# A two-block network on one core: the 32 x 32 inversions' data moved by TensorE, x normalized before its split, HGRN's levels copied under a mask

## The chip, the core and the metric

The kernel runs on one core of a Trainium2 chip. The metric is device time in microseconds of one execution: the median of the runs of the kernel before is 3642.4 us (three runs, 3641.06 to 3648.86 us). The engines are named as in the profile: PE is TensorE (PEld its weight loads), DVE is VectorE, ACT is ScalarE, POOL is GpSimd, SP is SyncE, which mostly issues DMAs. ACTq and SPq are DMA issues standing in the queues of ACT and SP.

## The reference

512 tokens of 1024 features pass through a first block (one layer, three branches) and a second block (two layers). The change touches the first block, up to the state space branch:

```
xn = rmsnorm(x, norm1_w);  p = xn @ w_in
z, xbc, dt, p_rwkv, p_hgrn, p_gate = split(p)
y_ssm  = ssd_branch(z, xbc, dt, ...) @ w_branch_ssm
y_rwkv = rwkv7_branch(p_rwkv, ...)   @ w_branch_rwkv
y_hgrn = hgrn2_branch(p_hgrn, ...)   @ w_branch_hgrn
mixed  = sigmoid(p_gate)[0] * y_ssm + [1] * y_rwkv + [2] * y_hgrn
x = x + mixed @ w_out;  then norm, feed-forward, norm, and the second block
# RWKV-7, per head of 64, both directions:
S_t = S_{t-1} diag(w_t) - (S_{t-1} kk_t)(kk_t a_t)^T + v_t k_t^T;  y_t = S_t r_t
# HGRN-2, per head of 128, both directions:
S_t = diag(f_t) S_{t-1} + (1 - f_t) v_t^T;  o_t = S_t^T q_t;  o = rmsnorm(o) * silu(g)
```

The kernel solves the RWKV recurrence in chunks of 64 tokens, for which it needs the inverse of a unit triangular 64 x 64 matrix (I + A) per chunk, head and direction: 32 of them in a tile of two heads.

## The kernel before, in words

All large products run on PE with the weights and the input each split into two float16 parts (three products for one). A 512 KB weight unit comes by DMA, ACT makes its high part (L1058 or L1054), DVE or POOL its low part (L1059, L1055).

`start` (L1374) loads x, and for each of its 8 tiles splits gain times x into the two parts xh and xl at once and adds up its squares. 1/rms comes out later: along the partitions as `rb`, by token as `rt`. The 1/rms is therefore multiplied into whatever the products give: in `conv_pad` (L247, DVE), in HGRN's q, k, i and g (L801, L806, L811, DVE), in the gates (L1310, POOL), in the z path of the state space branch.

The first layer (`first`, L914) has this order. RWKV (`rwkv`) is traced first, as foreground, four tiles j of two heads one after the other. For each, `rwkv_mid` (L396) makes G, all causal products of a chunk, under a mask; takes the 32 x 32 diagonal blocks of (I + A) out of G through a DRAM buffer `pd` into M, with a matrix per partition (issues L432, L441); inverts them by rows with DVE, in two independent chains of rows (L463 multiplies, L466 subtracts); sends the inverse X by DRAM buffer `pd2` back into G (L470, L473); and then completes the block above the diagonal with PE (L480 transposes, L485 and L490 products, copies by ACT and DVE to L491). `rwkv_scan` (L494) then walks over 8 chunks: PE products with the state z, DVE's L523 (minus the right side), PE by the inverse (L526), copies `uv`, and the next state: PE L533, DVE L541 adds the old state, DVE L542 multiplies by the decay. Inside chunk 2 of the scan, the next tile's projections (`rwkv_in`) are traced, inside chunk 4 its decays. `rwkv_out` (L555) ends a tile with a layer norm (PE transposes L580).

HGRN's four heads and 16 gate tiles are background: traced after RWKV in the order "hghhghgg" (h one head, g four gate tiles), with two PSUM banks "bg" of their own, and a scheduler moves their instructions into places where it expects engines to be idle. Each engine then executes its own list strictly in order. A head has seven levels, each with DVE products (L839, L840), PE products into the bank H (L845), and, for five of them, a DVE multiplication by a mask (L847) and a POOL addition (L848) into the score tile `hs`; then DVE's L859 and L860 for the next level.

When RWKV, the four heads and the 16 gates are through, the banks are given out again and the state space branch (`ssd`, L609, first product L625) begins, with one accumulator bank "acc"; its background is the two up projections of RWKV and HGRN, eight more gates and its own. Weight units come in two written lists, FOREGROUND and BACKGROUND.

## Time and profile before

| | us |
|---|---|
| median of three runs | 3642.4 |
| lowest and highest | 3641.06, 3648.86 |
| the profiled execution's span | 3644.9 |
| up to G of tile 0 (first L432) | 99.1 |
| RWKV's four tiles, to the last layer norm | 99.1 to 679.1 |
| first product of the state space branch | 687.6 |
| end of the state space branch, about | 985 |
| the rest: output, feed-forward, second block | 985 to 3644.9 |

A row of the timeline has a start, a duration, engine, line, operation, output<-input, how many run together, and in brackets the idle time before it with what ended it. In a view by line, the busy time and the mean length follow the bar, then the idle time before. A tile's name stands without its buffer number.

### The profile page before, as it was taken

Reading aid. Unit: us, or ns where it says so; the run is one execution under the profiler, and the core shown is the slowest. Engines: PE = TensorE matmul, PEld = TensorE weight load, DVE = VectorE, ACT = ScalarE, POOL = GpSimd, SP = SyncE. Lnnn points to the kernel's source line nnn. Section 1 sums busy time; section 2 is a strip of 40 time slices with the busy share of each in tenths; the row PEclk is TensorE's granted clock in tenths of the full one; section 3 lists DMA queues with packets and bytes.
Section 4 is the critical chain, followed back from the end, with each engine's and each line's share of the span. In section 5 each row is a group of like instructions: output and inputs, shape, how many; then the busy total and the mean of one; then the engine's idle time right before and its main releaser. Section 6 shows DMA issues by size and latency. Waiting matters only on the chain. (4 is left out here: it accounts for less than half of the span.)

```text
span 3644.9 us, 60827 instructions
## 1 busy us (share of the span) xinstructions
PE 3388.2 (93%) x23758; PEld 2045.0 (56%) x23758; DVE 2751.5 (75%) x5599; ACT 1624.4 (45%) x3033; POOL 751.7 (21%) x762
## 2 busy tenths in 40 slices
PE   7899898898899999999989999999999989999998
PEld 3566565554445567655545545568655545545567
DVE  6767867587577798688767677788688767767788
ACT  4232232455444444364456544444364456634344
POOL 1322223223332212101110131211101120132211
PEclk9897999999999999999999999999999999999999
DMA  4211212333352234322323353335322323353233
GB/s 137 70 49 40 64 40 63 131 111 113 106 171 94 97 99 142 108 74 75 106 76 100 106 170 99 98 112 159 106 73 72 105 81 101 108 172 123 94 99 98
DMA packets 151157, 368.17 MB, mean 101 GB/s; under 512 B 44098, under 2 KB 47428, under 8 KB 150868
## 3 DMA queue, kind: packets, MB, share of 16 engines
q1 hardware_dynamic: 117492, 336.03, 29.5%
q0 software_dynamic: 7680, 23.00, 1.9%
q10 hardware_dynamic: 25696, 5.25, 0.8%
q8 instruction: 186, 3.05, 0.3%
q14 instruction: 103, 0.84, 0.1%
HBM read 322.72 MB, written 40.04 MB: 100 GB/s over the span
## 5 line engine op out<-in xcount | busy, mean ns | idle before, releaser
L1169 PE MATMUL acc<-xh,whi 128*128 128x512 f16 x1224 | 469.3, 383 | 33.0 <-DVE w L753 11.8
L1171 PE MATMUL acc<-xh,wlo 128*128 128x512 f16 x1224 | 469.1, 383 | 20.6 <-DVE wlo L1059 20.3
L1170 PE MATMUL acc<-xl,whi 128*128 128x512 f16 x1224 | 469.6, 384 | 0.0
L1058 ACT ACTIVATE whi<-wst 128x1024 f16<-128x1024 f32 x240 | 250.0, 1049 | 263.4 <-PE acc L1170 141.7
L1059 DVE SCALAR_TENSOR_TENSOR wlo<-wst,whi 128x1024 f16<-128x1024 f32 x240 | 319.0, 1329 | 15.4 <-ACT whi L1058 14.9
L1169 PE MATMUL bg<-xh,bhi 128*128 128x512 f16 x788 | 311.1, 395 | 9.9 <-DVE hi L811 8.2
L1171 PE MATMUL bg<-xh,blo 128*128 128x512 f16 x788 | 310.5, 394 | 5.8 <-DVE reset L309 3.2
L1170 PE MATMUL bg<-xl,bhi 128*128 128x512 f16 x788 | 311.1, 395 | 0.0
L1171 PEld LDWEIGHTS <-wlo 128*128 128x128 f16 x1632 | 160.7, 98 | 232.5 <-DVE wlo L1059 46.4
L1170 PEld LDWEIGHTS <-whi 128*128 128x128 f16 x1632 | 160.5, 98 | 213.0 <-issue 41.6
L1169 PEld LDWEIGHTS <-whi 128*128 128x128 f16 x1632 | 161.1, 99 | 193.8 <-ACT whi L1058 13.5
L1428 POOL TENSOR_TENSOR w<-w,w 128x512 f32<-128x512 f32 x66 | 117.0, 1773 | 445.4 <-DVE w L1428 280.1
L1059 DVE SCALAR_TENSOR_TENSOR blo<-bst,bhi 128x1024 f16<-128x1024 f32 (+1 forms) x156 | 180.5, 1162 | 34.4 <-ACT bhi L1058 32.7
L1204 PE MATMUL acc<-whi,xh 128*128 128x128 f16 x1152 | 195.1, 219 | 2.1 <-DVE bias L1843 1.2
L1058 ACT ACTIVATE bhi<-bst 128x1024 f16<-128x1024 f32 (+1 forms) x156 | 136.4, 887 | 133.0 <-PE bg L1170 95.7
L1206 PE MATMUL acc<-whi,xl 128*128 128x128 f16 x1152 | 195.0, 219 | 0.0
L1205 PE MATMUL acc<-wlo,xh 128*128 128x128 f16 x1152 | 195.0, 219 | 0.0
L1171 PEld LDWEIGHTS <-blo 128*128 128x128 f16 x1172 | 117.0, 100 | 131.3 <-issue 16.3
L1170 PEld LDWEIGHTS <-bhi 128*128 128x128 f16 x1172 | 117.1, 100 | 130.7 <-issue 29.0
L1169 PEld LDWEIGHTS <-bhi 128*128 128x128 f16 x1172 | 117.3, 100 | 114.7 <-issue 15.1
L1204 PEld LDWEIGHTS <-xh 128*128 128x128 f16 x1408 | 139.9, 99 | 15.2 <-issue 5.0
L1205 PEld LDWEIGHTS <-xh 128*128 128x128 f16 x1408 | 140.0, 99 | 6.8 <-issue 5.0
(665 smaller groups left out, 9117.2 us busy)
## 6 DMA issues: line engine op xcount, KB each, us to landing
wst<-win SPq DMA_DIRECT2D x92, 512.0 KB, 3.6
bst<-win SPq DMA_DIRECT2D x64, 512.0 KB, 3.7
wst<-wff SPq DMA_DIRECT2D x60, 512.0 KB, 3.6
bst<-w SPq DMA_DIRECT2D x44, 512.0 KB, 3.5
gd<-bw SPq DMA_DIRECT2D x88, 256.0 KB, 2.1
ug<-gd SPq DMA_DIRECT2D x88, 256.0 KB, 2.7
wst<-w SPq DMA_DIRECT2D x34, 512.0 KB, 3.5
wst<-wf SPq DMA_DIRECT2D x30, 512.0 KB, 3.4
```

The source lines that it names most:

```text
L1058: nc.scalar.activation(out=hi[:, h], in_=st[:, h], func=AF.Copy, scale=WS)
L1059: nc.vector.scalar_tensor_tensor(out=lo[:, h], in0=st[:, h], scalar=WS, in1=hi[:, h], op0=ALU.mult, op1=ALU.subtract)
L1169: mm(ps, lhsT=wh, rhs=h[:, k, :], start=(k == 0), stop=False)
L1170: mm(ps, lhsT=wh, rhs=l[:, k, :], start=False, stop=False)
L1171: mm(ps, lhsT=wl, rhs=h[:, k, :], start=False, stop=(k == nk - 1))
L1204: mm(o, lhsT=xh, rhs=wh, start=(k == 0), stop=False)
L1205: mm(o, lhsT=xh, rhs=wl, start=False, stop=False)
L1206: mm(o, lhsT=xl, rhs=wh, start=False, stop=(k == 7))
L1428: tt = lambda eng, o, x, y, op=ALU.add: eng.tensor_tensor(out=o, in0=x, in1=y, op=op)
```

## The change

Six edits, all in the first block:

1. The inversion's data go by PE. G's 32 x 32 blocks are multiplied by parts of the identity into PSUM (64 products) and copied to M by four ACT copies. M and X now lie with the columns outside, so that a step along a row is 32 elements. The two chains become one, on all rows, with X padded by interleaved zero columns so that the rows of one half of the partitions count as even and the others as odd. X comes back by 16 products of 128 x 128 by 64 columns into PSUM, eight copies into G, and 32 small products with two copies into `st`, for which the transposes are gone. Both DRAM buffers and their DMAs are gone.
2. `start` adds up the squares first, then multiplies x by 1/rms (three tiles on POOL, five on DVE), then splits. What was multiplied by `rb` or `rt` later is now scaled by a constant, mostly in an ACT activation that reads PSUM.
3. HGRN's levels below the sixth: one predicated copy on DVE from PSUM into `hs` in place of the mask product and POOL's addition.
4. RWKV's old state is added in PSUM by a product with the identity; L523's work goes from DVE to ACT, and the two copies `uv` change engines.
5. The background is traced as "hhghghgg", its weight units with it.
6. The kernel is built with a DMA scratch size of 4096, and comments are gone, which moves line numbers.

```diff
 def conv_pad(self, ps, side):
-        nc.vector.tensor_tensor(out=xp[:, 2:T + 2], in0=ps, in1=self.rb, op=ALU.mult)
+        nc.scalar.activation(out=xp[:, 2:T + 2], in_=ps, func=AF.Copy, scale=IWS)
 def rwkv_mid(self, j):
-        pd = self.t(self.dram, [2, 32, 32, 32], "pd")
-        for q in range(2):
-            s = slice(32 * q, 32 * q + 32)
-            nc.scalar.dma_start(out=pd[q].rearrange("m i t -> i m t"), in_=G[s, :, s])
...
-            (nc.scalar, nc.sync)[q].dma_start(out=M[s], in_=pd.rearrange("q m i t -> (q m) i t"))
+        for u in range(2):
+            ps = self.b("S")
+            for t in range(16):
+                for q in range(2):
+                    s = slice(32 * q, 32 * q + 32)
+                    mm(ps[s, 32 * t:32 * t + 32], lhsT=G[:, :, 32 * q + 16 * u + t], rhs=self.ident[:, s], start=True, stop=True)
+            for h in range(2):
+                nc.scalar.copy(out=M[64 * h:64 * h + 64, 512 * u:512 * u + 512], in_=ps[0:64])
...
         for i in range(31):
...
-            for c, n in rs:
-                v.tensor_tensor(out=t, in0=X[c][:, 0:n, i:i + 1]..., in1=M[:, i:i + 1, ts]..., op=ALU.mult)
-            for c, n in rs:
-                v.tensor_tensor(out=X[c][:, 0:n, ts], in0=X[c][:, 0:n, ts], in1=t, op=ALU.subtract)
-        pd2 = self.t(self.dram, [2, 32, 8, 2, 2, 32], "pd2")
...
-        for q in range(2):
-            s = slice(32 * q, 32 * q + 32)
-            nc.scalar.dma_start(out=G[s, :, s], in_=pd2[q].rearrange("m r c e t -> (r c e) m t"))
+            v.tensor_tensor(out=t, in0=Xv[:, rs, i:i + 1]..., in1=Mv[:, i:i + 1, ts]..., op=ALU.mult)
+            v.tensor_tensor(out=Xv[:, rs, ts], in0=Xv[:, rs, ts], in1=t, op=ALU.subtract)
+        for k in range(8):
+            for h in range(2):
+                mm(px[:, 64 * k:64 * k + 64], lhsT=X[:, o:o + 128], rhs=self.ident[:, 64 * h:64 * h + 64], start=(h == 0), stop=(h == 1))
+        for k in range(4):
+            for q in range(2):
+                if q:
+                    nc.scalar.copy(out=dst, in_=src)
+                else:
+                    v.tensor_copy(out=dst, in_=src)
+        for i in range(32):
+            mm(pt[i // 16][0:32, ...], lhsT=Xv[:, i // 2 * 2 + 1], rhs=self.ident[:, 64 * (i % 2):64 * (i % 2) + 32], start=True, stop=True)
+        nc.scalar.copy(out=st[:, 0:16], in_=pt[0][0:32]...)
+        v.tensor_copy(out=st[:, 16:32], in_=pt[1][0:32]...)
...
-                nc.tensor.transpose(px[lo, 32 * n:32 * n + 32], G[lo, m, lo], self.ident[lo, lo])
-            nc.scalar.copy(out=st[lo], in_=px[lo])
 def rwkv_scan(self, j):
-            v.tensor_scalar(out=wn[lo], in0=pw[lo, 0:256], scalar1=-1.0, scalar2=None, op0=ALU.mult)
+            nc.scalar.activation(out=wn[lo], in_=pw[lo, 0:256], func=AF.Copy, scale=-1.0)
-            v.tensor_copy(out=uv[0][lo, chs[0]], in_=pu[lo, 0:128])
-            nc.scalar.copy(out=uv[1][lo, chs[1]], in_=pu[lo, 128:256])
+            nc.scalar.copy(out=uv[0][lo, chs[0]], in_=pu[lo, 0:128])
+            v.tensor_copy(out=uv[1][lo, chs[1]], in_=pu[lo, 128:256])
+                    if z is not None:
+                        mm(o, lhsT=self.ident, rhs=z[:, d], start=True, stop=False)
-                    v.tensor_tensor(out=zf, in0=z.rearrange("p d k -> p (d k)"), in1=pz[:, 0:256], op=ALU.add)
-                    v.tensor_tensor(out=four_v(zf), in0=four_v(zf), in1=zb, op=ALU.mult)
+                v.tensor_tensor(out=zn..., in0=pz[:, 0:256]..., in1=zb, op=ALU.mult)
 def ssd(self, yh, yl):
-            v.tensor_tensor(out=z, in0=pz, in1=self.rb, op=ALU.mult)
-            nc.scalar.activation(out=th, in_=z, func=AF.Tanh, scale=0.5)
-            v.scalar_tensor_tensor(out=z, in0=th, scalar=1.0, in1=z, op0=ALU.add, op1=ALU.mult)
+            nc.scalar.activation(out=z, in_=pz, func=AF.Tanh, scale=0.5 * IWS)
+            v.scalar_tensor_tensor(out=z, in0=z, scalar=1.0, in1=pz, op0=ALU.add, op1=ALU.mult)
 def hgrn(self, yd):
-            v.tensor_tensor(out=q, in0=self.fmx(it), in1=self.rb, op=ALU.mult)
+            nc.scalar.activation(out=q, in_=self.fmx(it), func=AF.Copy, scale=IWS)
...
-                    v.tensor_tensor(out=t, in0=po..., in1=hm[:, l:l + 1]..., op=ALU.mult)
-                    nc.gpsimd.tensor_tensor(out=sc, in0=sc, in1=t, op=ALU.add)
+                    v.copy_predicated(sc, hm[:, l:l + 1].bitcast(U16)..., po...)
 def first(self, next_gain):
-                for s in "hghhghgg":
+                for s in "hhghghgg":
 def gates(self, name, u0, n, gd, g0=0):
-                nc.scalar.copy(out=g, in_=ps)
-                nc.gpsimd.tensor_tensor(out=g, in0=g, in1=self.rb, op=ALU.mult)
+                nc.scalar.activation(out=g, in_=ps, func=AF.Tanh, scale=0.5 * IWS)
 def start(self, gain):
-                self.norm_tile(k, x[:, k], gain)
-            self.norm_end()
+                self.square_sums(k, x[:, k], None, eng=nc.vector)
+            self.norm_end(1.0)
+            for k in range(8):
+                (nc.gpsimd if k % 3 == 1 else nc.vector).tensor_tensor(out=x[:, k], in0=x[:, k], in1=self.rb, op=ALU.mult)
+                self.split(self.xh[:, k, :], self.xl[:, k, :], x[:, k], self.col(gain, k))
```

How the scheduler's lists move with it is shown at three places.

DVE in the first inversion, before: tx and X with their numbers are the products and rows of the two chains, M the matrix; L811 is an HGRN head's.

```order
L811 TENSOR_TENSOR hi_3874<-bg_3883,rt_15_148 128x512
L463 TENSOR_TENSOR tx_111_559<-X_113_561,M_558 128x29
L463 TENSOR_TENSOR tx_112_560<-X_114_562,M_558 128x27
L466 TENSOR_TENSOR X_113_561<-X_113_561,tx_111_559 128x29
L466 TENSOR_TENSOR X_114_562<-X_114_562,tx_112_560 128x27
L263 TENSOR_SCALAR i_1038<-i_1038 128x512
```

There a subtraction never stands right behind the product that it needs. The same place near the first inversion's end, after: L464 and L465 are the product and the subtraction of the one chain, L818, L827, L841 and L848 an HGRN head's, L1059 a weight's low part.

```order
L464 TENSOR_TENSOR tx_634<-X_635,M_563 128x78
L465 TENSOR_TENSOR X_635<-X_635,tx_634 128x13x6
L464 TENSOR_TENSOR tx_634<-X_635,M_563 128x70
L818 SCALAR_TENSOR_TENSOR hg_4083<-hg_4083,bg_4091 128x512
L465 TENSOR_TENSOR X_635<-X_635,tx_634 128x14x5
L827 TENSOR_TENSOR hs_4197<-H_4192,ident_75 128x512
L464 TENSOR_TENSOR tx_634<-X_635,M_563 128x56
L841 TENSOR_TENSOR hw_4212<-hq_3860,hp_3902 128x2x128x2
L465 TENSOR_TENSOR X_635<-X_635,tx_634 128x14x4
L1059 SCALAR_TENSOR_TENSOR blo_4382<-bst_4379,bhi_4381 128x512
L464 TENSOR_TENSOR tx_634<-X_635,M_563 128x45
L848 COPY_PREDICATED hs_4197<-hgm_3845,H_4204 128x512
```

Each pair is now dependent, and the background's operations stand between the two of a pair. 62 operations of the chain take the place of 120 small ones in pairs.

PE from RWKV's last layer norm (L580, its transposes) to the first product of the state space branch (L625), before; the rows with bg are background products.

```order
L580 MATMUL T_3726<-ident_75,M_3408 128x128
L1171 LDWEIGHTS blo_6349
L1171 MATMUL bg_6383<-xh,blo_6349 128x512
L1169 LDWEIGHTS bhi_6348
L1169 MATMUL bg_6383<-xh,bhi_6348 128x512
...
L1170 MATMUL bg_6420<-xl,bhi_6386 128x512
L1171 LDWEIGHTS blo_6387
L1171 MATMUL bg_6420<-xh,blo_6387 128x512
L625 LDWEIGHTS xh
```

Here 42 background products of 512 columns stand between the layer norm's first transpose and L625. After, a part of the same stretch, which ends at L631 (the same product as L625 above); L1204 to L1206 are products of HGRN's i and g by token, L825 the first of its score products.

```order
L1206 LDWEIGHTS xl
L1206 MATMUL bg_5904<-bhi_5792,xl 128x128
L825 MATMUL H_6005<-hq_5680,hw_6003 128x128 x4
L1169 LDWEIGHTS bhi_5898
L1169 MATMUL bg_6190<-xh,bhi_5898 128x512
...
L1170 MATMUL bg_6438<-xl,bhi_6406 128x512
L1171 LDWEIGHTS blo_6407
L1171 MATMUL bg_6438<-xh,blo_6407 128x512
L631 LDWEIGHTS xh
```

The stretch now holds 315 background products of 512 columns, 192 of 128 columns and 82 of an HGRN head's scores and states. RWKV's four tiles hold 57, 20, 125 and 83 background products in place of 128, 112, 126 and 192.

DVE from the last layer norm to the state space branch, before: L568 and L574 belong to the norm, L582 to the tile's gate, L614 and what follows to the state space branch.

```order
L568 TENSOR_SCALAR rs_658_3709<-mv_649_3684 128x8
L574 TENSOR_SCALAR M_3408<-M_3408,mv_649_3684,rs_658_3709 128x64 x8
L582 TENSOR_SCALAR w_3731<-T_3726,cols_77 128x512
L614 TENSOR_SCALAR dsk_6480<-cols_77 128x8
L1223 SCALAR_TENSOR_TENSOR w_3736<-w_3731,w_3735 128x512
```

All four heads have ended ahead of it. After, L574 and L580 are the norm's, L885 to L908 the end of the third head, and L811, L841 and L848 the fourth head, whose levels run on to the branch's first row.

```order
L574 TENSOR_SCALAR rs_646_3813<-mv_637_3788 128x8
L580 TENSOR_SCALAR M_3506<-M_3506,mv_637_3788,rs_646_3813 128x64 x8
L885 COPY hst_5498<-H_5494 128x128
L908 TENSOR_TENSOR hw_5524<-hw_5524,hg_5244 128x512
L811 TENSOR_SCALAR hp_5715<-hk_5716,hc_655_3848,hc_654_3847 128x512
...
L841 TENSOR_TENSOR hw_6025<-hq_5680,hp_5715 128x2x128x2
L848 COPY_PREDICATED hs_6010<-hgm_3845,H_6017 128x512
...
L620 TENSOR_SCALAR dsk_6496<-cols_77 128x8
```

So a whole head and the end of another moved behind RWKV's last tile. From the first block's feed-forward on, the lists of DVE, ACT and POOL are the same before and after.

## Rows read from the trace of the kernel before

**Rows 1.** Windows by stage: length, busy time (x instructions) of PE, PEld, DVE, ACT, POOL, granted clock

```profile
541.10:676.00 134.90, 114.29 (x949) 76.73 (x947) 88.18 (x251) 41.66 (x91) 43.77 (x29) 0.92 0.21 61
676.00:688.00 12.00, 11.46 (x47) 5.39 (x48) 5.46 (x13) 5.32 (x10) 4.74 (x9) 0.84 0.57 180
```

**Rows 2.** Timeline of the second tile's inversion: start, length, engine, line, operation

```profile
244.47 0.31 ACTq L432 DMA_DIRECT2D pd<-G  x1
256.65 0.28 DVE L463 TENSOR_TENSOR tx<-X,M 128x31 f32<-128x31 f32 x2
290.42 0.17 DVE L466 TENSOR_TENSOR X<-X,tx 128x8 f32<-128x8 f32 x1
295.31 0.93 ACTq L473 DMA_DIRECT2D G<-pd  x2
305.24 0.94 PE L485 MATMUL S<-w,G 32*32 32x32 f32 x24
314.51 0.57 ACT L491 COPY G<-S 32x512 f32<-32x512 f32 x1 [1.03 <-PE S L490]
381.79 0.28 DVE L551 TENSOR_TENSOR M<-M,S 64x128 f32<-64x128 f32 x1 [0.32 <-PE S L550]
```

**Rows 3.** Timeline, the same issue L432 in the first and the last tile

```profile
99.15 0.96 ACTq L432 DMA_DIRECT2D pd<-G  x2
541.06 0.31 ACTq L432 DMA_DIRECT2D pd<-G  x1
```

**Rows 4.** Waits of ACT, 0 to 692: total us, times, longest

```profile
ACT w L482 <- PE S L480: 64.9, 4, 26.5
```

**Rows 5.** Groups by line, 0 to 692: busy us, mean ns, idle before

```profile
L466 DVE TENSOR_TENSOR X<-X,tx 128x54 f32<-128x54 f32 (+13 forms) x240 | 48.8, 242 | 0.0
L463 DVE TENSOR_TENSOR tx<-X,M 128x54 f32<-128x54 f32 (+13 forms) x240 | 47.5, 237 | 0.0
L541 DVE TENSOR_TENSOR z<-z,S 128x256 f32<-128x256 f32 x24 | 10.0, 419 | 13.6 <-PE S L533 13.5
L848 POOL TENSOR_TENSOR hs<-hs,hw 128x512 f32<-128x512 f32 x20 | 36.0, 1800 | 73.4 <-DVE hw L847 48.6 <-DVE X L466 24.8
```

**Rows 6.** Line L1623, durations in ns min/median/max: half of its reads are strided

```profile
L1623 DVE TENSOR_TENSOR w<-acc,rb x16: 691/863/1052, 1780.8 to 3110.9; 128x512 f32<-128x512 f32 x16
```

**Rows 7.** Timeline of DVE: L257 needs L256's output, L1059 needs neither

```profile
104.30 0.74 DVE L256 SCALAR_TENSOR_TENSOR fr<-xp,cols,fr 128x512 f32<-128x512 f32 x1
105.07 0.75 DVE L257 SCALAR_TENSOR_TENSOR fr<-xp,cols,fr 128x512 f32<-128x512 f32 x1
105.74 1.22 DVE L1059 SCALAR_TENSOR_TENSOR wlo<-wst,whi 128x1024 f16<-128x1024 f32 x1
```

**Rows 8.** Timeline of PE: pace of products of 512 and of 128 columns

```profile
978.04 0.38 PE L1171 MATMUL bg<-xh,blo 128*128 128x512 f16 x1
978.25 0.38 PE L1169 MATMUL bg<-xh,bhi 128*128 128x512 f16 x1
102.56 0.22 PE L1204 MATMUL bg<-bhi,xh 128*128 128x128 f16 x1
102.62 0.22 PE L1205 MATMUL bg<-blo,xh 128*128 128x128 f16 x1
```

**Rows 9.** Timeline of PE: the last layer norm and the state space branch's first product

```profile
679.13 0.42 PE L580 MATMUL T<-ident,M 128*128 128x128 f32 x1
687.60 0.19 PE L625 MATMUL acc<-wdh,xh 128*128 128x32 f16 x1
```

**Rows 10.** Timeline of DVE: one level of an HGRN head to the next

```profile
152.59 0.68 DVE L839 TENSOR_TENSOR hw<-hq,hp 128x512 f32<-128x512 f32 x1
157.80 0.68 DVE L839 TENSOR_TENSOR hw<-hq,hp 128x512 f32<-128x512 f32 x1
```

**Rows 11.** Timeline, 10 to 40 us: the first use of the first product

```profile
37.54 0.69 DVE L247 TENSOR_TENSOR xp<-acc,rb 128x512 f32<-128x512 f32 x1 [1.00 <-PE acc L1171]
```

**Rows 12.** Waits of PE in the state space branch, 692 to 985: total us, times, longest

```profile
PE acc L1169 <- DVE w L753: 11.8, 5, 3.8
```

More of the change, by code (lines that the diff above doesn't have):

```diff
@@ L13 @@
 BF16 = mybir.dt.bfloat16
+U16 = mybir.dt.uint16
 AF = mybir.ActivationFunctionType
@@ L475, in rwkv_mid @@
+        for i in range(32):
+            mm(pt[i // 16][0:32, 32 * (i % 16):32 * (i % 16) + 32], lhsT=Xv[:, i // 2 * 2 + 1], rhs=self.ident[:, 64 * (i % 2):64 * (i % 2) + 32], start=True, stop=True)
+        nc.scalar.copy(out=st[:, 0:16], in_=pt[0][0:32].rearrange("p (i m) -> p i m", m=32))
+        v.tensor_copy(out=st[:, 16:32], in_=pt[1][0:32].rearrange("p (i m) -> p i m", m=32))
+        st = M[0:32].rearrange("p (m i) -> p m i", i=32)
         lo, hi = slice(0, 32), slice(32, 64)
@@ L631, in ssd @@
         for i in range(4):
-            v.scalar_tensor_tensor(out=da[:, i], in0=pd[:, 32 * i:32 * i + 32], scalar=self.rt[:, i:i + 1], in1=self.row("dtb"), op0=ALU.mult, op1=ALU.add)
+            v.scalar_tensor_tensor(out=da[:, i], in0=pd[:, 32 * i:32 * i + 32], scalar=IWS, in1=self.row("dtb"), op0=ALU.mult, op1=ALU.add)
         v.tensor_scalar(out=fl(da), in0=fl(da), scalar1=-1.0, scalar2=None, op0=ALU.mult)
```

73 lines of the change are left out of this document (32 added, 41 removed), and 2 rows, old and new, of the table BACKGROUND.

## The prediction

> **What bounds the kernel now.** I read the windows by stage first, then the timeline of one RWKV tile, then the waits and the groups by line in 0 to 692 us, and last the two lists of instructions side by side. Everything that changes lies ahead of about 985 us; behind it the lists of DVE, ACT and POOL are the same, so the prediction is a sum over RWKV's four tiles, the stretch between them and the state space branch, and that branch.
>
> In an RWKV tile no engine is full: in the last one DVE is busy 88 of 135 us and PE 114, and PE's busy time counts background products and a granted clock of 0.92 [rows 1]. A chain bounds it. A tile takes (541.06 - 99.15) / 3 = 147.3 us [rows 3]. In the second, the way from G into the inversion takes 244.47 to 256.65, 12.2 us, the inversion to 290.6, 33.9 us, the way back until the products above the diagonal begin 14.6 us (290.6 to 305.24), those products to 315.1, 9.9 us, the scan to 382.1, 67 us; another 15 us go by until the next tile's G [rows 2]. While the inversion runs, ACT's queue stands behind the DMA issues: four waits of 65 us in all, the longest 26.5 us [rows 4]. Behind the last tile little is left: from the last transpose of its layer norm to the state space branch's first product 679.13 to 687.60, 8.5 us [rows 9].
>
> **The tile, part by part.** Into M: both DMA legs (12.2 us) give way to 64 products of 32 columns and four copies. The nearest row has 24 such in 0.94 us, 0.039 each [rows 2], so 2.5 us; at the pace of 128-column products, 0.06 [rows 8], 3.8. The last two copies are 1.1 us by L491's 0.57 [rows 2], and I allow 1 to 2 us for the hand-overs between engines: about 5.7, a gain of 6.5 (4 to 8).
>
> The inversion: 120 operations become 62 with the same elements, 2856 of each kind in a tile. In the trace they are busy (48.8 + 47.5) / 4 = 24 us a tile [rows 5]; the two shortest forms, of 8 and 31 elements a row, run at 0.17 and 0.14 us [rows 2], so most of it is a fixed price, and 58 operations at 0.06 to 0.11 give back 3.5 to 6.4 us. Two things take from it. The steps are now 32 elements apart. The nearest row is L1623, of whose 16 executions 8 read in steps of 64 elements: 0.69 us without and 1.05 us with them [rows 6], 0.7 ns more for an element; 2 x 2856 x 0.7 is 4 us (6 if the write pays too). And each operation needs the one in front. A dependent pair has a pitch of 0.77 us where the next, independent one has 0.67 [rows 7]; 62 x 0.10 is 6.2 us at most, less where background stands between the two. Last, POOL gives back ground: its additions L848, 36 us, go [rows 5], so that fewer of DVE's operations run beside one of POOL's, which may help and is priced by no row here. I take 0 for the inversion, from -6 to +6.
>
> The Trainium skill (page "SBUF — State Buffer", section "Door 1: The DMA port swizzle (why `[64,N]` ≈ `[32,N]`)") says that an access which crosses into another 16-byte line pays a penalty and that four fp32 are what can be strided over freely: a rule against this change. By it every element of the strided operands would pay; the 0.691 and 1.052 us above agree in sign. By the rule with its penalty on reads and writes alike the 6 us hold rather than the 4, and the sum is 8 us later. The page "VectorE: DVE Perf Modes", section "The DRAIN you can't avoid", says that an operation does not begin until the one before has left the pipe, in which case two independent chains bought nothing; by it the 6.2 us would be 0, the inversion some 4 us shorter in a tile, and the sum 15 us earlier. The pitches of 0.77 and 0.67 do not bear it out fully, and the sum goes by them.
>
> Back from X: four DMAs out, two in, transposes and a copy (14.6 us) give way to 16 products of 64 columns (0.08 each by the pace above, 1.3 us), eight copies on two engines (4 x 0.57 at most, 2 us), 32 products of 32 columns (1.2), a copy (0.6) and hand-overs (1): 6, a gain of 8.5 (6 to 10). The products above the diagonal lose the second half's transposes and copy: 2 of 9.9 us (0 to 3).
>
> The scan: the old state's addition L541, 0.42 us, leaves the chain in six chunks [rows 5], with a dependent step 6 x 0.5 = 3 us; the two products that replace it are due before the chain's own and hide behind the waits for `uv` (if not, 12 x 0.06 to 0.16 us, at most 2). L523's move to ACT is even: ACT is free, with the DMAs out of its queue. More comes from PE: the list puts 285 background products of 512 columns into the four tiles where 558 stood, and at 0.215 us each [rows 8] that is 59 us less PE work, 15 a tile, of which most was in the scans and part in the chain's way. I take 10 us in all (4 to 14). The projections' `conv_pad` on ACT instead of DVE (0.69 us [rows 11], three a tile), and the rest: 2.5 us (0 to 4).
>
> Sum: 6.5 + 0 + 8.5 + 2 + 10 + 2.5 = 29.5 us a tile. Over the way from the first L432 to the last layer norm, 3.85 tiles' worth of 147 us by rows 3 and 9 less the start, that is 114 us. `start` normalizes x before its split, but the first projection no longer waits for `rb` at 37.54 [rows 11]: I take 3 us earlier (from 3 later to 4). The last layer norm's transpose moves from 679 to about 562.
>
> **What comes behind.** What left the tiles has not left the program. 315 background products of 512 columns at 0.215 us are 67.9 us, 192 of 128 columns at 0.055 to 0.06 are 11, 82 for HGRN at 0.06 to 0.16 are 9: 88 us of PE time (84 to 93) where 42 products stood [rows 8]. They are in PE's list ahead of the state space branch, and so must all end before it. In them runs HGRN's fourth head, whose levels took 5.2 us each [rows 10], seven levels and the parts around them about 50 us, with 2 to 15 products between the levels; I add 15 us for PE's waits on it: 103 (85 to 118). The branch then begins at 562 + 103 = 665 in place of 687.6, 23 us earlier.
>
> In the branch itself 12 `conv_pad` and one operation of the z path leave DVE, which PE waited for 11.8 us [rows 12]; but the single accumulator bank is now held until DVE has read it behind ACT's tanh. I take 4 us less (from 10 less to 8 more). HGRN's predicated copies and scaled activations shorten work that is not on the chain, except in the fourth head. The scratch size I cost at nothing, since no step of the chain hangs on it (2 us either way).
>
> Together: 23 + 4 = 27 us off the profiled 3644.9, 3618. That execution is 2.5 us above the median of the three runs, so 3616.
>
> The break-even lies at a gain per tile of (103 - 8.5 - 3 - 4) / 3.85 = 23 us.
>
> **The rivals.** Faster: the tile shortens by 38 (the upper ends of the scan and of the way into M and back, 5 us from the inversion), 146 us in all, and the stretch behind takes the 88 of PE's work and no more: 679 - 146 - 3 + 88 = 618, 70 us early, with the branch's 4 that is 3571. For it speaks that POOL's slowing of DVE goes; against it that half-full PE has a granted clock of 0.92 and 0.84 in these stretches [rows 1], which less background would not raise.
>
> Slower: the inversion on strided columns costs 5 us more instead of 0, since every one of 62 operations pays for step and dependence, and the scan gives only the 4 us of its addition. The tile then shortens by 6.5 - 5 + 8.5 + 2 + 4 = 16 us, 62 in all, and the stretch behind is still 103: 679 - 62 - 3 + 103 = 717, 29 us late, 3671 with the branch's 4 off less the 2.5. It decides from the 23 us per tile above. Speaking for it: a background that once filled the waits of a chain is now run by itself.
>
> It doesn't do what it says: the waits on the DMAs are hidden behind other work of the chain, and moving them by PE changes nothing. ACT's four waits and the empty 12 and 15 us in the timeline [rows 2, 4] speak against; it would give about 3642.
>
> **Chances.** The forecast 0.48, with 3595 to 3637 as its own range; faster rival 0.22 (3555 to 3595); slower rival 0.27 (3637 to 3690); no effect 0.03. The range, 3560 to 3665, leaves out the far ends of both rivals. A measurement tells 0.2%, 7.3 us, from no change: faster than 3635 are the fast rival and 0.40 of the forecast, 0.62; within 0.2% the forecast's last 0.08, the slower rival's first 0.04 and the no-effect case, 0.15; slower 0.23.
>
> **What would show it.** In the profile after: the way from G to the inversion's first operation 5 to 7 us, and from its last to the products above the diagonal about 6; ACT's 26 us waits gone. The inversion's length, 28 to 40 us, tells the strided price. The last layer norm's transposes at 545 to 580, the branch's first product at 650 to 680, and between them PE over 80% busy. It is wrong if a tile still takes over 125 us, if PE waits over 25 us for HGRN's last head, or if the branch takes more than its 297 us.

## The result and the profile after

The changed kernel takes 3673.6 us, the median of six runs (3665.7 to 3698.4), the kernel before in the same rounds 3644.5: a ratio of 1.0088, with a 95% interval of 1.0060 to 1.0117. It is slower by some 29 us where 27 us less were forecast, and it lies beyond the range of 3560 to 3665. The profiled execution spans 3676.5 us.

The windows of the changed kernel by stage, cut at its own four tiles (each from the first of its G products) and at the last layer norm's transposes. The columns are those of [rows 1]: the busy time of PE, PEld, DVE, ACT and POOL, the granted clock of TensorE, the busy share of the DMA engines and the GB/s that they moved.

```profile
95.40:226.70 131.30, 120.99 (x1113) 90.10 (x1112) 92.38 (x191) 41.82 (x90) 20.80 (x21) 0.90 0.09 29
226.70:347.10 120.40, 111.43 (x1078) 83.30 (x1077) 80.28 (x196) 41.69 (x93) 19.02 (x21) 0.96 0.09 32
347.10:480.50 133.40, 124.20 (x1055) 85.53 (x1054) 93.41 (x216) 48.02 (x107) 25.62 (x23) 0.97 0.13 45
480.50:601.50 121.00, 110.38 (x1114) 85.74 (x1114) 79.58 (x204) 35.85 (x79) 24.07 (x18) 0.96 0.08 27
601.50:704.30 102.80, 97.25 (x675) 56.69 (x676) 53.97 (x82) 38.45 (x74) 29.23 (x23) 1.00 0.40 138
```

And of the kernel before, cut at the same places:

```profile
87.40:228.20 140.80, 125.72 (x982) 83.03 (x982) 104.30 (x275) 41.08 (x92) 40.65 (x37) 0.92 0.20 57
228.20:380.60 152.40, 141.38 (x1057) 97.90 (x1056) 107.23 (x304) 42.18 (x92) 36.00 (x37) 0.85 0.16 42
380.60:519.90 139.30, 128.42 (x1032) 86.64 (x1031) 112.06 (x301) 44.34 (x97) 42.23 (x36) 0.95 0.21 60
519.90:676.30 156.40, 133.98 (x1037) 90.44 (x1036) 100.62 (x292) 44.02 (x95) 50.49 (x33) 0.88 0.20 57
676.30:687.60 11.30, 11.27 (x47) 5.28 (x47) 4.76 (x12) 4.81 (x9) 4.61 (x8) 0.84 0.56 178
```

The tiles went from 147.2 to 126.5 us in the mean, 82.8 us in all. The stretch behind them went from 11.3 to 102.8 us, 91.5 more, and the first tile begins 8.0 us later (95.4 for 87.4). So the state space branch starts 16.7 us later: the first product at 704.34 for 687.60 [rows 9].

```profile
602.88 0.27 PE L586 MATMUL T<-ident,M 128*128 128x128 f32 x1
704.34 0.18 PE L631 MATMUL acc<-wdh,xh 128*128 128x32 f16 x1
```

From there to the end it is 2972.2 us for 2957.3, and the branch itself has no part in that. Up to the row of 1/rms behind it (`rbs`) it takes 276.9 us for 278.7:

```profile
965.60 0.69 DVE L1297 COPY rbs<-T 128x512 f32<-128x512 f32 x1 [1.04 <-PE T L1296]
980.52 0.69 DVE L1297 COPY rbs<-T 128x512 f32<-128x512 f32 x1 [1.64 <-PE T L1296]
```

The rest, where the lists of DVE, ACT and POOL are the same, is 2695.3 us for 2678.6. Ten traces looked at, of these two kernels and of eight below, have 2678.6 to 2695.3 there, with before's the shortest and the change's the longest: e_rm below, whose ACT list behind the branch is the change's instruction for instruction, has 2685.3. So these 17 us are the spread of single traces and aren't shown to belong to the change. Of the 29 us between the medians, 16.7 are seen ahead of the branch, and where the others come from stays open. The 16.7 is itself a difference of two single traces: the kernel before with nothing but another scratch size began its branch 7 us earlier.

The second tile, as in [rows 2]: M's copies, the inversion from L464 to L465, the products above the diagonal L494 to L500, the scan's last addition L557.

```profile
245.90 1.17 ACT L438 COPY M<-S 64x512 f32<-64x512 f32 x2 [0.68 <-PE S L436]
247.10 0.21 DVE L464 TENSOR_TENSOR tx<-X,M 128x31 f32<-128x31 f32 x1 [3.09 <-ACT M L438]
285.67 1.26 DVE L465 TENSOR_TENSOR X<-X,tx 128x16 f32<-128x16 f32 x1
293.75 1.19 PE L494 MATMUL S<-M,G 32*32 32x32 f32 x32
301.03 0.57 ACT L500 COPY G<-S 32x512 f32<-32x512 f32 x1 [1.74 <-PE S L499]
348.01 0.28 DVE L557 TENSOR_TENSOR M<-M,S 64x128 f32<-64x128 f32 x1 [0.74 <-PE S L556]
```

The way back is 6.9 us for 14.6, the inversion 39.8 for 33.9, the scan 46.7 for 67. But the scan's pair of numbers sets a scan at one granted clock against a scan at another. The first two scans, before and then after the change:

```profile
173.60:229.90 56.30, 55.64 (x407) 39.06 (x406) 34.41 (x81) 23.34 (x66) 15.71 (x12) 1.00 0.13 43
315.10:382.10 67.00, 66.25 (x425) 48.30 (x423) 40.79 (x92) 20.44 (x59) 13.98 (x11) 0.80 0.03 9
```

```profile
165.30:227.90 62.60, 58.47 (x389) 43.83 (x388) 33.01 (x71) 20.92 (x58) 9.84 (x7) 0.84 0.03 9
301.60:348.30 46.70, 46.70 (x391) 36.72 (x389) 23.15 (x57) 17.47 (x49) 2.12 (x1) 1.00 0.06 22
```

Before's second scan, the one that the forecast read, ran at a granted clock of 0.80, and its first at 1.00; in the change it is the other way round. At 0.97 to 1.00, before has scans of 56.3, 55.9 and 53.3 us, the change 46.7, 47.7 and 48.6, 5 to 10 us less; and each kernel has one slower scan, of 67.0 and 62.6 us. In the mean it is 58.1 and 51.4.

ACT's wait L482 of [rows 4] is gone. In its place stands a smaller one: the eight copies back into G were to run on two engines at once, and run in turn.

```profile
ACT G L480 <- DVE G L482: 28.0, 11, 7.2
```

The groups by line, 0 to 704 us, to [rows 5]: half the inversion's operations with 90.2 us of busy time for 96.3, and the predicated copy in place of GpSimd's 36 us.

```profile
L465 DVE TENSOR_TENSOR X<-X,tx 128x126 f32<-128x126 f32 (+22 forms) x124 | 47.8, 385 | 2.5
L464 DVE TENSOR_TENSOR tx<-X,M 128x126 f32<-128x126 f32 (+22 forms) x124 | 42.4, 342 | 9.1 <-ACT M L438 6.8
L848 DVE COPY_PREDICATED hs<-hgm,H 128x512 f32<-128x512 uint16 x20 | 14.5, 725 | 2.2 <-PE H L847 1.9
```

### The profile page after: what moved, and what is told of

It reads as the page before. It is cut to its first block, busy times and chain, and to the rows that moved or that the text cites. A ratio compares the mean times of both kernels' runs of the same rounds, so it can differ in the third digit from the quotient of the medians.

```text
span 3676.5 us, 62122 instructions
## 1 busy us (share of the span) xinstructions
PE 3420.7 (93%) x24622; PEld 2086.6 (57%) x24622; DVE 2715.8 (74%) x5282; ACT 1657.0 (45%) x3103; POOL 691.4 (19%) x709
## 5 line engine op out<-in xcount | busy, mean ns | idle before, releaser
L1171 PE MATMUL acc<-xh,wlo 128*128 128x512 f16 x1224 | 470.3, 384 | 21.6 <-DVE wlo L1059 21.6
L1059 DVE SCALAR_TENSOR_TENSOR wlo<-wst,whi 128x1024 f16<-128x1024 f32 x240 | 318.2, 1326 | 32.4 <-ACT whi L1058 24.7
L1059 DVE SCALAR_TENSOR_TENSOR blo<-bst,bhi 128x1024 f16<-128x1024 f32 (+1 forms) x156 | 182.6, 1174 | 48.3 <-ACT bhi L1058 46.1
L1204 PE MATMUL acc<-whi,xh 128*128 128x128 f16 x1152 | 195.1, 219 | 1.9 <-DVE bias L1845 1.3
L1206 PE MATMUL acc<-whi,xl 128*128 128x128 f16 x1152 | 195.0, 219 | 0.0
L1169 PEld LDWEIGHTS <-bhi 128*128 128x128 f16 x1172 | 116.7, 100 | 115.1 <-issue 12.3
L1204 PEld LDWEIGHTS <-xh 128*128 128x128 f16 x1408 | 139.3, 99 | 12.8 <-issue 3.4
```

Source lines behind the costliest of these rows:

```text
L1059: nc.vector.scalar_tensor_tensor(out=lo[:, h], in0=st[:, h], scalar=WS, in1=hi[:, h], op0=ALU.mult, op1=ALU.subtract)
L1169: mm(ps, lhsT=wh, rhs=h[:, k, :], start=(k == 0), stop=False)
L1171: mm(ps, lhsT=wl, rhs=h[:, k, :], start=False, stop=(k == nk - 1))
L1204: mm(o, lhsT=xh, rhs=wh, start=(k == 0), stop=False)
L1206: mm(o, lhsT=xl, rhs=wh, start=False, stop=(k == 7))
```

## The experiments

Each kernel's edit stands against before or after. "The branch" is the state space branch's first product, taken from the trace.

**One edit at a time, on the kernel before.** Each also has the scratch size.

```diff
 p1: rwkv_mid as after the change, all else as before
 p2: start, conv_pad, hgrn's q, k, i, g, gates, ssd's z as after
 p4: rwkv_scan as after
 p3: hgrn's copy_predicated
 p5: "hhghghgg" and its units (without the scratch size)
 p6: dynamic_dma_scratch_size=4096 alone
```

> The kernel before with the inversion's data moved by TensorE alone (and the scratch size of 4096, which its tiles need). Theory 1 (the sum of a chain in RWKV's tiles and of what is left behind them): the tiles shorten by 14 to 17 us each, some 60 us in all; the order leaves 192 background products of 512 columns and 53 of 128 behind the last tile in place of 42, 40 to 45 us with the waits; start unchanged. The state space branch begins at about 670, the kernel takes 3625 to 3635. Theory 2 (the stretch follows TensorE's work, which the small products raise by 4 to 5 us a tile): the branch begins at 700 to 710 and the kernel takes 3660 to 3667.

Measured: 3697.8 us, ratio 1.0154 (1.0137 to 1.0171), the branch at 731.2. Both theories missed. The tiles took 139 us in the mean instead of 130, since the inversions grew to 42 to 59 us: in the mean 26 us of each (19 to 36) are taken by other DVE operations that the list now puts between the chain's. Behind the tiles stand 80 us. The fourth head's closing operations begin at 714.1, and the branch follows 17 us later.

> The kernel before with RWKV's old state added in PSUM and the right side's negative on ScalarE alone (and the scratch size). Theory 1: a scan shortens by 3 to 7 us, 12 to 28 in all, but the order leaves 192 background products of 512 columns, 116 of 128 and 80 of a head's behind the last tile in place of 42, 45 us more: the branch begins 15 to 30 us later, 3660 to 3675. Theory 2 (48 more products of 128 columns, about 5 us of TensorE's work): 3648 to 3652.

Measured: 3716.2 us, ratio 1.0206 (1.0190 to 1.0222), the branch at 747.8, the latest of the single edits. Its scans are hardly shorter (54.0 for 58.1 us in the mean); the list moves HGRN behind the tiles, and the last head's end is 19 us ahead of the branch:

```profile
728.62 0.69 DVE L904 TENSOR_TENSOR hw<-H,s 128x512 f32<-128x512 f32 x1 [1.13 <-POOL s L1223]
```

> The kernel before with x normalized ahead of its split alone (with all scaled activations that follow from it, and the scratch size). Theory 1: the first tile's products G begin 5 to 9 us later than at 87.4, since TensorE stands idle until x has gone through DVE and GpSimd a second time, and the tiles give little of it back: 3645 to 3655. Theory 2 (TensorE's work, which is unchanged): no difference, 3644 within 4 us.

Measured: 3649.5 us, ratio 1.0018 (1.0006 to 1.0030). The first G products come at 96.7, 9.3 us later, as theory 1 had it; the inversions fall to 25 to 32 us, and the branch comes at 681.7.

> The kernel before with HGRN's levels copied under the mask alone (and the scratch size). GpSimd's 20 additions and 20 DVE products go for 20 predicated copies of the same length. Theory 7 (the chain stays, the background's own chain shortens by about 2.5 us a level and DVE runs undisturbed by GpSimd): the branch at 670 to 682, 3625 to 3637. If the heads' chain is hidden by the tiles anyway: 3640 to 3648.

Measured: 3647.3 us, ratio 1.0016 (1.0006 to 1.0026). The second theory's time, the first one's start of the branch, 678.3. That start decides nothing: the next run shows one as early with the lists unchanged.

> The kernel before with the background in the order of the change alone (two heads first). The list has 144, 146, 115 and 188 background products in the tiles and 79 behind them, in place of 42. If the background's own progress sets the end: within 10 us of before's 687.6, 3635 to 3655. If a later place of the gates costs its own price: 8 us later, 3650 to 3658.

Measured: 3654.2 us, ratio 1.0038 (1.0026 to 1.0051), the branch at 690.0.

> The kernel before with the scratch size of 4096 alone; the lists of all engines stay as they are. If it costs nothing, as the forecast said: the ratio's interval takes in 1, the state space branch begins within 2 us of 687.6. If software DMAs pay for it: 3648 to 3655, all of it behind the start of the branch.

Measured: 3639.4 us, ratio 0.9997 (0.9983 to 1.0010). It costs nothing, but the branch came at 680.4 with the lists unchanged: a single trace's start of the branch is good to about 7 us. Of the 7.2 us, 4.8 lie in the second tile's scan, which took 62.2 us at a granted clock of 0.86 for 67.0 at 0.80. The starts of p2, p3 and p5 don't differ from before's by more than that.

The single edits don't add up: by the medians against before's in the same rounds (p1, p4, p2, p3, p5, p6) 55, 74, 7, 4, 13 and -2 us make 151, and together they make 29.

**Without one edit.** The changed kernel without the normalization:

> The changed kernel without the normalization ahead of the split and what follows from it (1/rms multiplied in later, as before). The list behind the last tile stays much the same (303 products of 512 columns and 192 of 128). Theory 3: the first G products come 5 to 8 us earlier, the state space branch is 5 to 12 us shorter, GpSimd's and DVE's operations for 1/rms come back in the heads (5 a head): 3655 to 3668. If the normalization helps in the tiles more than it costs at the start and in the branch: 3680 or more.

Measured: 3672.2 us, ratio 1.0089 (1.0062 to 1.0117), as the whole change. The start is 2.4 us earlier, not 5 to 8: its list puts 164 background products ahead of the first G, the change's 98. The inversions are 1.5 us longer, the tiles the same (126.5 us in the mean), but 115.2 us stand behind them for 102.8, and the branch begins at 714.1.

**The stride.** M and X row by row, with the way back column by column:

```diff
-        Xv = X[:, 0:1024].rearrange("p (t r) -> p r t", r=32)
+        Xv = X.rearrange("p (r t) -> p r t", t=32)
-                mm(px[:, 64 * k:64 * k + 64], lhsT=X[:, o:o + 128], ...)
+                for a in range(4):
+                    mm(px[32 * a:32 * a + 32, 64 * k:64 * k + 64], lhsT=Xv[:, 1 - h:33 - h, 4 * k + a], ...)
```

> The changed kernel with M and X row by row, so that DVE's 62 operations of an inversion read and write neighbouring elements; the price is 64 products of 32 by 64 in place of 16 of 128 by 64 on the way back, and a permuting copy on ScalarE. Theory 1: the operations lose 0.6 ns an element, 3.4 us a tile, their own share of an inversion falls from 22 to about 19 us, and the branch begins 6 to 12 us earlier, 3660 to 3668. If the stride is not what lengthens them (only dependence and fixed price): their share stays at 22 and the time within 4 us of the changed kernel's. Theory 2 (2.5 us more of TensorE's work a tile): 3680 to 3685.

Measured: 3694.3 us, ratio 1.0137 (1.0114 to 1.0160), the branch at 735.6. The largest operation, of 136 elements, falls from 0.384 to 0.301 us, 0.61 ns an element, as expected; but the list changed again. The inversion's own operations are busy 17.6 us for 22.5, and yet the inversions gave back only 1.1 us of their 39.6, since DVE now idles 6.7 us in each for 2.3. The four tiles are 19 us longer and the stretch behind them 11. What the stride costs is shown; that it is worth its price here is not.

**The place of the background.** One head and four gates traced behind each inversion, or at each tile's end, instead of all behind RWKV:

```diff
             self.rwkv_mid(j)
+            behind(("hg", "hg", "hg", "hg")[j])     # e_mid, b_mid; e_end: behind rwkv_out
```

> The changed kernel with the background traced by tile: one HGRN head and four gate tiles behind each tile's inversion, in place of all of them behind RWKV. The list then holds 232, 164, 170 and 100 background products of 512 columns in the four tiles and none behind the last (the changed kernel: 57, 20, 125, 83, and 315 behind). Theory 3 (the place in the list decides, the work fits into the waits of RWKV's chain): tiles of 125 to 140 us, nothing of a head behind the last, the state space branch begins at 620 to 665 and the kernel takes 3585 to 3635. Theory 4 (the background's work costs the same wherever it stands): the tiles grow by what the tail loses, 145 to 155 us each, the branch begins at 690 to 710, 3660 to 3680.

Measured: 3710.2 us, ratio 1.0191 (1.0166 to 1.0216). Nothing is left behind the tiles (9.5 us), and the branch comes at 751.7 all the same: the tiles took 147 to 181 us, more than theory 4 had it, with scans of 84.7 us in the mean for 51.4. Theory 3 falls. Its third tile:

```profile
414.50:595.70 181.20, 170.21 (x1320) 116.88 (x1319) 103.80 (x233) 55.71 (x119) 31.82 (x26) 0.86 0.13 45
```

> The same with head and gates traced at each tile's end: 69 products of 512 columns and 64 of a head's stand behind the last tile. Theory 3: a tail of 25 to 35 us, the branch at 635 to 680, 3600 to 3650. Theory 4: 3660 to 3680.

Measured: 3721.2 us, ratio 1.0220 (1.0167 to 1.0273), the branch at 776.4. The tiles took 139 to 178 us, and 46.7 us stand behind them.

> The kernel before with the background traced by tile in the same way, as a control: its list was even already (128, 112, 126, 192 products and 42 behind). Theory 3: little to win, 3630 to 3655, so that a gain of the run above would belong to the six edits. If tracing by tile is a gain by itself, whatever the edits: 3600 to 3620.

Measured: 3696.2 us, ratio 1.0151 (1.0122 to 1.0180), the branch at 735.3. On the kernel before, too, an even spread by tracing costs 55 us (3641.3 in the same rounds), with scans of 70.2 us in the mean for 58.1. That the background's products stand ahead of the chain's there and delay it is likely, but these runs don't show it by itself.

**The chain alone.** HGRN's heads and 16 gates left out of both kernels, and RWKV left out of the changed one:

```diff
-                for s in "hhghghgg": ...
+                (zeros by DMA into gd[8:24] and yd[1])
```

> The kernel before with the background up to the state space branch left out: HGRN's four heads and the 16 gate tiles of RWKV and HGRN are not computed, zeros stand in their place. It shows the chain of RWKV's tiles alone. Theory 5 (the DMA round trips were the room in which the background ran; a line through the tiles of all runs with DMAs has 121 us at no background and half a microsecond for each of background): tiles of 115 to 125 us, the branch's first product at 570 to 605. Theory 6 (the tiles' chain is hardly longer than the changed kernel's, and the background's place alone makes the difference): tiles under 105 us.

> The changed kernel with the same work left out. Theory 5 (a line through the tiles of all runs without DMAs has 90 us at no background, and 1.1 us for each of background): tiles of 85 to 95 us, 26 to 35 shorter than before's without background, the first product of the branch at 450 to 480. Theory 6: 95 to 105 us, within 10 us of before's.

> The changed kernel with RWKV left out (zeros in its place); HGRN's heads and the gates stand alone ahead of the state space branch. Theory 5: they take 240 to 300 us by themselves; with the 365 of the chain alone and the start that is nearly the whole 704, so that almost nothing of the two overlaps in the changed kernel, while the kernel before hid 80 to 120 us of it. Theory 6 (a fourth head alone is late): under 200 us.

Each was executed once. Measured: the branch at 652.0 and 641.7. Before's second and last tile, and the changed kernel's:

```profile
224.80:370.50 145.70, 113.75 (x599) 75.44 (x598) 67.34 (x244) 24.36 (x57) 12.24 (x20) 0.59 0.09 22
512.80:643.50 130.70, 85.75 (x505) 69.38 (x503) 45.94 (x225) 14.60 (x41) 8.93 (x7) 0.50 0.06 13
```

```profile
222.30:363.10 140.80, 129.07 (x816) 92.20 (x815) 67.17 (x173) 33.51 (x75) 11.69 (x17) 0.62 0.04 14
504.30:633.30 129.00, 101.13 (x720) 86.02 (x719) 47.97 (x158) 22.06 (x56) 8.96 (x7) 0.53 0.01 3
```

Tiles of 137.4 us in the mean for before, 135.5 for the change. Both theories' lengths are wrong, and the difference is 1.8 us a tile. The column to read is the granted clock: 0.50 to 0.62, mostly the lower level. The background alone puts the branch at 311.7, about 275 us behind its first products' use, as theory 5 had it (240 to 300); but its 365 us for the chain alone became 542, from 91.2 to 633.3.

**One chain or two.** The merged rows split again into two independent halves, with and without background:

```diff
-            t = tx[:, 0:n * nt] ...; rs = slice(1, i // 2 * 2 + 2, 2)
+            rs = [(c, (n + 1 - c) // 2, slice(1 + 2 * c, 2 * n, 4)) for c in range(2) if n > c]
+            for c, m, q in rs: (product into tx[c])   for c, m, q in rs: (subtraction)
```

> The same without the background (HGRN's heads and 16 gates left out, zeros in their place). Theory 7: the last tile's inversion, where DVE does nothing else, takes 16 to 18 us (one chain: 21.5; before's two: 15.4), and the branch begins 12 to 24 us earlier than at 641.7. Rival 8: 20 to 22 us, and no earlier than 635.

Measured: the branch at 628.2, 13.5 us earlier. First and last operation of the last tile's inversion, where DVE does nothing else, in before, the change, and the change with two chains, all without background:

```profile
539.49 0.29 DVE L463 TENSOR_TENSOR tx<-X,M 128x31 f32<-128x31 f32 x2 [7.62 <-DMA M<-pd]
554.68 0.17 DVE L466 TENSOR_TENSOR X<-X,tx 128x8 f32<-128x8 f32 x1
```

```profile
526.68 0.21 DVE L464 TENSOR_TENSOR tx<-X,M 128x31 f32<-128x31 f32 x1 [2.06 <-ACT M L438]
548.07 0.18 DVE L465 TENSOR_TENSOR X<-X,tx 128x16 f32<-128x16 f32 x1
```

```profile
516.26 0.33 DVE L466 TENSOR_TENSOR tx<-X,M 128x31 f32<-128x31 f32 x2 [2.06 <-ACT M L438]
534.45 0.17 DVE L469 TENSOR_TENSOR X<-X,tx 128x8 f32<-128x8 f32 x1
```

They last 15.4, 21.6 and 18.4 us: of the 6.2 that the change adds, two chains give back 3.2, and the 3.0 left is near to 2 x 2856 strided elements at 0.61 ns, 3.5. A little above theory 7's 16 to 18, below rival 8's 20.

> The changed kernel with the inversion's rows in two independent chains again (every other of the odd rows each), all else as changed; the same elements in 120 operations in place of 62. Theory 7 (dependence is what the merged chain pays: pitch 0.365 us an operation against 0.127 with two chains): the chain's own share of an inversion falls from 22 to 16 to 18 us, 16 to 24 us over the stage if the list stays, 3650 to 3662. Rival 8 (the stride pays): own share 20 to 22, 3668 to 3680. A list that moves background anew can shift either by 30 us; then the own share decides.

Measured: 3675.4 us, ratio 1.0097 (1.0071 to 1.0124). The four tiles fell from 506 to 470 us and the branch did not move, 704.6. What the tiles lost stands behind them, 141.2 us: the list has 360 background products of 512 columns there for 315.

```profile
445.20:563.40 118.20, 109.97 (x990) 81.05 (x990) 71.19 (x243) 39.12 (x91) 24.99 (x18) 0.91 0.13 42
563.40:704.60 141.20, 130.76 (x980) 81.01 (x981) 80.24 (x123) 48.12 (x91) 41.76 (x33) 0.98 0.34 114
```

**The clock.** Idle products in the scans of the changed kernel without background:

```diff
+            self.warm(3)      # three products xh' x xh of 512 columns, ahead of wn, uv and py in each chunk
```

> The changed kernel without background, but with nine idle products of 512 columns a chunk in the scans, whose result nobody reads (72 a tile, 15.5 us of TensorE at full pace). If the tiles' 129 to 141 us are long because TensorE is granted 0.5 to 0.6 of its clock there: granted clock over 0.8 in the scans, scans of 46 to 58 us in place of 63 to 70, though more work is done. If the clock doesn't matter: scans of 70 to 85 us, longer by the work added.

Measured: the branch at 589.9 in place of 641.7, with 62 us more work (288 x 0.2155). The scheduler drew the products forward: 42 and 39 of them lie in the first two scans, none in the last two. All 288 ran between 30.6 and 366.5 us, 78 of them ahead of the first G. The four scans:

```profile
149.50:195.70 46.20, 46.20 (x328) 32.90 (x326) 19.86 (x51) 14.96 (x46) 0.00 (x0) 1.00 0.00 1
255.90:319.20 63.30, 63.30 (x331) 43.31 (x331) 23.39 (x56) 15.02 (x45) 1.27 (x1) 0.73 0.00 1
383.70:454.40 70.70, 68.44 (x293) 50.41 (x293) 23.35 (x56) 15.15 (x46) 1.26 (x1) 0.52 0.00 1
512.20:575.40 63.20, 58.41 (x271) 48.20 (x270) 9.81 (x31) 11.22 (x37) 0.00 (x0) 0.50 0.00 1
```

The first scan has more to do than the third and takes 46.2 us for 70.7, at a granted clock of 1.00 for 0.52. Without the idle products it took 68.0 at 0.50:

```profile
156.10:224.10 68.00, 65.27 (x284) 50.31 (x285) 20.25 (x51) 15.11 (x45) 0.00 (x0) 0.50 0.00 1
```

The whole first tile, at 1.00 with 108 idle products recorded in it, took 105.0 us for 131.1. No such run was made of the kernel before.

**A version that beats both.** Edits 2, 3 and 6 on the kernel before, with the z path's scaled product copied out of PSUM at once:

> The kernel before with x normalized ahead of its split and HGRN's levels copied under the mask (and the scratch size), with the DMAs of the inversion and RWKV's addition as before; in the z path ScalarE copies the scaled product out at once, so that the accumulator bank is not held behind the tanh. Theory 5 (the room stays, the background becomes cheaper for DVE and GpSimd): inversions of 25 to 32 us, the branch at 670 to 682 in spite of a start 8 us later, 3620 to 3640. If what the first edits cost at the start decides: 3645 to 3655.

Measured: 3640.6 us over 12 runs for 3647.3, ratio 0.9984 (0.9975 to 0.9994), the branch at 675.7. The inversions took 25 to 32 us, as expected; the gain is 0.2%, and it is the only one found.

## Why the prediction was wrong

By its own steps, from the traces, means of the four tiles in us; the last column is the same difference without background. "Into M" runs from the first DMA issue (before) or the first product (after) to the inversion's first operation:

| step | forecast | measured | without background |
|---|---|---|---|
| into M | -6.5 | 12.2 to 5.8: -6.5 | -7.4 |
| inversion | 0 | 34.6 to 39.6: +5.0 | +7.2 |
| back from X | -8.5 | 15.0 to 6.5: -8.6 | -3.4 |
| products above the diagonal | -2 | 9.9 to 7.8: -2.1 | -1.5 |
| scan | -10 | 58.1 to 51.4: -6.7 | +1.6 |
| G and the rest | -2.5 | -1.9 | +1.6 |
| a tile | -29.5 | 147.2 to 126.5: -20.7 | -1.8 |
| start | -3 | +8.0 | -2.9 |
| behind the tiles | 11.3 to 106 | 11.3 to 102.8 | none left out there |

Against the forecast of 3618 the profiled execution is 58.5 us too long. The tiles make some 31 us of it and the start 11, less about 3 for the stretch behind: 39 us ahead of the branch. The other 19 lie behind its start. There the forecast had 4 us less, the branch itself gave 1.8, and the rest is the spread of traces told above; "if the branch takes more than its 297 us" did not come true, "if a tile still takes over 125 us" did.

**What failed.** Two terms of the sum "6.5 + 0 + 8.5 + 2 + 10 + 2.5 = 29.5 us a tile" and the term for the start. The 0 for the inversion measured 5.0 us longer, and 7.2 with no background near it, where the chain's dependence makes some 3 us and the stride about as much ("One chain or two" above). The 10 for the scan measured 6.7, and nothing (1.6 longer) without background at the lower clock. The 3 us earlier for the start measured 8.0 later.

The stretch behind came out as forecast, but partly by luck: from the norm's last transpose, 101.5 us measured (602.88 to 704.34) for 103. TensorE is busy 97.3 us of the window instead of 88, and idle 5.6 instead of 15. HGRN's 82 fp32 products are recorded as 164 of 0.11 us, 18 us where the forecast had 9.

The start had the wrong sign. After the change each of the eight tiles of x passes DVE or GpSimd a second time before TensorE can multiply it:

```profile
29.35 0.59 PE L1169 MATMUL acc<-xh,whi 128*128 128x512 f16 x1 [3.99 <-ACT xh L1219]
40.84 0.60 ACT L248 ACTIVATE xp<-acc 128x512 f32<-128x512 f32 x1 [1.43 <-PE acc L1171]
```

The first use of a product is at 40.84 for 37.54 [rows 11]. Before, 24 background products ran from 20.83 us on, ahead of the first foreground product at 32.16; now the first product of all is the one at 29.35. The forecast looked at when the first result may be used, not at when the first can be computed. p2, with the normalization alone, has 9.3 us of delay. The lists have a part in it too: without the normalization (m2) the change begins only 2.4 us earlier, and p1, which has none, begins its first G at 93.7.

By the forecast's own break-even, 23 us a tile with the start 3 us earlier, the tiles' 20.7 us don't pay for the stretch behind; the start's 11 us of error come on top. That is the slower rival's outcome, and its 3671 lies near the measured time in part by luck. It had the inversion's 5 us right, but a tile's gain at 16 us (20.7) and the branch at 717 (704.3), no error at the start, and nothing of the 17 us of spread behind the branch. (Its sum gives 3668, not 3671: the branch's 4 us are already in the forecast's 3618. The faster rival's gives 3569.) Its reasons were only half right: the inversion's own share of DVE is 22.7 us (22.1 before), and most of its 5 us are other operations in the list, 16.7 us for 12.3, of which the third tile alone has 29.9.

But the runs without background show more. Of the 20.7 us, 1.8 belong to the chain, at the lower clock that both had there (the last section says what that leaves open). The rest, by subtraction, goes with the background that has left: by the lengths in the traces the four tiles hold 137 us of its TensorE work in place of 223, 22 us a tile less, and the tail 97 in place of 9. No run took work from the background alone, so this share is argued and not shown. The forecast set the departed work down as the tail, 88 us, and allowed 15 us a tile of it for the scan; but it also took the other stretches of the trace, 33.9 us of inversion and 14.6 us of way back, as lengths of the chain. They were lengths under load. Undisturbed, before's inversion lasts 20.8 us in the mean and its way back 9.9. So at the lower clock the DMA trips saved by TensorE were worth 7.4 + 3.4 us, not 15, and merging the chains took 7.2 of them.

The clock moved as well. The forecast's argument against the faster rival was that less background would not raise it; in the change's tiles it was 0.90 to 0.97 and 1.00 behind them, for before's 0.85 to 0.95 and 0.84.

On the merged chain the forecast set 3.5 to 6.4 us of gain against 6 to 10 of loss and took 0. Two pairs of rows show the sum, the dependent chain of the change and the two chains of before, both without background (x2 are two operations run together):

```profile
535.12 0.38 DVE L465 TENSOR_TENSOR X<-X,tx 128x133 f32<-128x133 f32 x1
535.54 0.37 DVE L464 TENSOR_TENSOR tx<-X,M 128x126 f32<-128x126 f32 x1
535.95 0.37 DVE L465 TENSOR_TENSOR X<-X,tx 128x126 f32<-128x126 f32 x1
```

```profile
545.13 0.34 DVE L466 TENSOR_TENSOR X<-X,tx 128x60 f32<-128x60 f32 x2
545.39 0.37 DVE L463 TENSOR_TENSOR tx<-X,M 128x76 f32<-128x76 f32 x2
```

A dependent operation starts its whole length plus 0.03 us behind the one before (0.373 us for a length of 0.339); an independent one starts before that one has ended: 0.126 us apart in the median where each lasts 0.208. In the last tile, where DVE does nothing else, the 119 steps of two chains cost less than the 61 of one (15.4 and 21.6 us). The Trainium skill (page "VectorE: DVE Perf Modes", section "The DRAIN you can't avoid") has the next operation wait for an empty pipe and adds that one that is not held starts earlier; the prediction took the first half alone, and the independent pairs here, 0.126 us apart for a length of 0.208, agree with the second. The Trainium skill's page "SBUF — State Buffer", section "Door 1: The DMA port swizzle (why `[64,N]` ≈ `[32,N]`)", with its penalty for stepping over lines, is borne out by the 0.61 ns an element.

What remains open: why the list of a single edit costs 55 or 74 us. In both, the fourth head ends late, 714 and 729, and the branch follows it by 17 and 19 us. In the change, two chains took 36 us from the tiles, and the head's end stayed where it was, in the change and with two chains:

```profile
684.39 0.69 DVE L907 TENSOR_TENSOR hw<-H,s 128x512 f32<-128x512 f32 x1 [1.13 <-POOL s L1226]
684.67 0.69 DVE L911 TENSOR_TENSOR hw<-H,s 128x512 f32<-128x512 f32 x1 [1.13 <-POOL s L1230]
```

That the background's own progress sets the branch's start in these kernels would fit them all, but it is not shown. In before, e_mid and b_mid the branch comes 43 to 66 us behind the head's end; and a stretch full of TensorE's work, 97.3 of 102.8 us in the change, would put head and branch together too, while in p1 and p4 TensorE is busy only 66 and 69 of 80 us there. No run took work from the background alone. Fixing one list and changing only an edit's cost was not possible, as the scheduler rewrites the list.

## What to carry to other kernels

The length of a step in a trace under load is not what its removal is worth: first take the load away, in both versions, and compare the chains, with the granted clock beside each. Where background work fills a chain's waits, removing a wait can remove its place too, so the sum has to follow the background to where it goes. Two short dependent chains side by side can beat one with half the operations, and an even spread of background products in the order of tracing can cost more than a tail.

## What the runs showed of the hardware

That leaving work out makes the rest slower was not expected: scans of 63 to 70 us at a granted clock of 0.50 to 0.52 without background, 46.2 with 42 idle products in them at 1.00, and with 62 us of useless work added, the branch came 52 us earlier. In these runs the chain of small products alone did not hold TensorE at its upper level of 2.4 GHz; with background between them the scans had 0.80 to 1.00. It also says how far the comparison without background reaches: both kernels ran near the lower level of 1.2 GHz there. In the first tile of the kernel with idle products, at 1.00, the way into M took the same 5.1 us, the way back 5.7 for 7.0 and the scan 46.1 for 68.0, so TensorE's steps cost less at the upper level than the last column of the table has them. What before's would cost there was not measured, so the chains are compared at the lower level only, and by single executions.
